# Delta-rule products and value transposes put down later, half pages kept out of the residual's buffers

## The chip, the core and the metric

One core of one Trainium2 chip runs the whole program. TensorE (PE) multiplies matrices, VectorE (DVE) and ScalarE (ACT) do elementwise work, GpSimd (POOL) helps, and SyncE (SP) issues nearly all DMAs between the chip's memory (HBM) and on-chip memory. Each engine runs its own instructions in order and waits on semaphores for the others; a DMA whose buffer is still in use holds up every later DMA of SP. The metric is the device time of one execution, as a median of several.

## The reference

The program is two transformer blocks over x of 1024 tokens by 1024 features, in fp32. The change lies in the first block and in what that block's buffers do later; the first block is, cut to its core:

```python
mod = cond @ w_ada + b_ada                       # cond = silu(c), six rows of 1024
sh_a, sc_a, gt_a, sh_f, sc_f, gt_f = split(mod, 6)
h = x * (1 + sc_a) + sh_a
q, k, v, z, a, b, gl_q, gl_k, gl_v, gl_g, gl_r = split(h @ w_in)
o_dn  = gated_delta_rule(l2(q), l2(k), v, ...)   # 4 heads of 128, chunks of 64
o_gla = gla_attention(...)                       # 4 heads
y = concat(gate(o_dn, z), gate(o_gla, gl_g)) @ w_o
x = layer_norm(ALPHA * x + (1 + gt_a) * y, ln1_g, ln1_b)
h = x * (1 + sc_f) + sh_f
u = causal_dwconv(h @ w_up, conv_w) + conv_b     # 1024 -> 2 * 2816, then 3 taps along time
y = (silu(gate) * val) @ w_down
x = layer_norm(ALPHA * x + (1 + gt_f) * y, ln2_g, ln2_b)
```

The delta rule solves, for each chunk of 64 tokens, a unit lower triangular system with I + M. The kernel inverts the 16x16 diagonal blocks first and then doubles the block size twice.

## The kernel before

**Products.** Every large product in fp32 is done as three products of a rounded high part and a remainder: ACT writes the high part (L430), DVE subtracts it to get the low part (L433, `split`), and PE runs three matmuls (`mm3`, through `mm` at L415; transposes are at L419). Weights come by DMA in blocks of 256 or 512 KB, the modulation's w_ada in pieces of 128x512.

**What sets the order.** The host program writes the instructions with a planner (`Order`). Work is split into generators. `yield t` says that what follows is due t planner microseconds later; a generator that is due goes ahead of the main stream of products. `yield self.need(n)` makes a generator wait until n pages of on-chip memory are free. What comes out is one fixed list of instructions per engine.

**Pages.** `Arena` hands out pages of 1024 columns (`full`) and halves of them (`half`). A caller can name pages that it would rather not have (`away`). In `half`, that list counts only if a new page has to be cut; a half that is already free is handed out, whatever page it is from. Two groups matter here: the eight pages `ypages` (named `y` in the trace), which hold rows of the residual and then of the mixer's output, and five pages `dset`, on which the FFN's product streams its weights.

**Around the change.**
- `mod_rest` (L881) makes eight pieces of the modulation rows while the mixer runs: for a piece, eight loads of w_ada (L891) into three halves, eight accumulating DVE operations (L900, the first L902), and then either a reshaping to columns or a product with a column of ones; for the gate rows the sum goes to HBM (gta_d, gtf_d; L916) through the first of these halves.
- `delta` (L1442) prepares one head, inverts its 16x16 blocks in 15 short pairs of DVE operations (L1541, L1543, L1546), writes the inverse and its transpose to HBM (t_d, L1547; u_d, L1548), and starts `delta_levels` (L1604) for each half of the sequence. That reads both back (L1613, L1614) and doubles the block size with small fp32 matmuls (128x64 results).
- `mix_op` (L1687) claims the `ypages`, loads the mixer's eight rows mix_d (L1695, 512 KB each), and transposes them for the output product.
- `st_up` (L1911) is the FFN's first product, in Strassen steps of twelve matmuls. It keeps four steps of split weights ready in a ring; weights come by L1931 into pages of `dset`, and each pair of weight blocks takes one half page for a temporary: `tmp[q] = A.half(self.dset)` (L1938). ACT copies the result of the first step of a block into a page (L1996), later steps are added by DVE (L1998 to L2007). `unit_out` and the convolution (L2044 to L2049, L2108, L2136) then work on it and store to s_d.
- `res_rows` (L1784) runs beside it as a generator of its own: it builds the residual rows of the second layer norm. Its loop is

```python
        for t in range(8):
            yield self.need(1)
            pg = A.full()
            x, rows = pg.ap, slice(t * P, (t + 1) * P)
            nc.sync.dma_start(x, self.xh_d[rows, :])
            yield 7
            # twice: x *= ln1_g row, yield 3.5, x += ln1_b row, yield 3.5
            nc.sync.dma_start(self.res_d[rows, :], x)
            A.give(pg)
```

(load L1797, DVE L1801 and L1803 twice each, store L1805). The two layer-norm rows hold two pages of their own until the loop ends.

Of the kernel before, what the change touches and what calls it, by code (L numbers as in the profile page):

```python
# [99 lines left out]
class Arena:  # L100
# [14 lines left out]
    def full(self, away=()):  # L115

        for a in (list(away) + self.avoid, self.avoid):
            for i, p in enumerate(self.free):
                if p not in a:
                    return self.free.pop(i)  # L120
        return self.free.pop(0)

    def half(self, away=()):
        if not self.hfree:
            p = self.full(away)
            p.subs = [Page(p.ap[:, 0:512], p, 0), Page(p.ap[:, 512:1024], p, 1)]
            self.hfree += p.subs
        return self.hfree.pop(0)

    def give(self, *xs):  # L130
# [39 lines left out]
def p3(ap, b=P):  # L170
    return ap.rearrange("p (a b) -> p a b", b=b)
# [6 lines left out]
class Down:  # L178
# [23 lines left out]
    def load(self):  # L202
        K = self.K
        A, q = K.A, K.nc.sync
        mine = lambda: [p for p in A.free if p in K.dset]
        while len(self.gp) < 4 and mine():
            pg = A.full([p for p in A.free if p not in K.dset])
            self.gp.append(pg)
            self.gb += [pg.ap[:, 0:512], pg.ap[:, 512:1024]]

        while self.gi < min(len(self.steps), self.at + len(self.gb)):
            c, p, k = self.steps[self.gi]
            q.dma_start(self.gb[self.gi % 8], K.s_d[self.chunks[c][k], :, SLOT[p]])
            self.gi += 1
        while self.want and mine():
            c, x, k = key = self.want.pop(0)
            self.pg[key] = A.full([p for p in A.free if p not in K.dset])
            if x != "t":
                q.dma_start(self.pg[key].ap, self.src(2 * self.chunks[c][k] + (x == "w1")))
        ok = lambda p: p in K.dset and p not in K.dn  # L220
        while not self.want and self.more and any(ok(p) for p in A.free):
            x, f = key = self.more.pop(0)
            pg = K.tail[key] = A.full([p for p in A.free if not ok(p)])
            q.dma_start(pg.ap, K.g_d[f] if x == "g" else self.src(f))
# [86 lines left out]
class Kern:  # L311
# [569 lines left out]
    def mod_rest(self, cond):  # L881
        nc, I, A = self.nc, self.I, self.A
        V = nc.vector
        self.gta_d = self.dram.tile([1, D], F32, name="gta_d")
        self.gtf_d = self.dram.tile([1, D], F32, name="gtf_d")
        self.mcol2 = self.const.tile([P, 16], F32, name="mcol2")
        for c in range(4, 12):
            yield self.need(0, 4)
            ah, *wh = [A.half() for _ in range(4)]
            acc = ah.ap  # L890
            load = lambda k: nc.sync.dma_start(wh[k % 3].ap, I["w_ada"][0, k * P:(k + 1) * P, c * 512:(c + 1) * 512])  # L891
            load(0)
            load(1)
            for k in range(KT):
                yield 5.5
                if k + 2 < KT:
                    load(k + 2)
                a = wh[k % 3].ap
                if k:
                    V.scalar_tensor_tensor(acc, a, cond[:, k:k + 1], acc, op0=OP.mult, op1=OP.add)  # L900
                else:
                    V.tensor_scalar(acc, a, cond[:, 0:1], None, op0=OP.mult)  # L902
            A.give(*wh[1:])
            yield 2
            if c // 2 in (3, 4):
                self.mod_cols(acc, self.mcol2[:, 4 * (c - 6):4 * (c - 5)], 4 * c, 4)
            else:
                dst = self.gta_d if c // 2 == 2 else self.gtf_d
                br = wh[0].ap[0:1, :]
                nc.sync.dma_start(br, I["b_ada"][0:1, c * 512:(c + 1) * 512])  # L910
                yield 2.66
                ps = self.ps()
                self.mm(ps[:1, :], self.ones[:, 0:1], acc, True, True)
                V.scalar_tensor_tensor(br, ps[:1, :], 1.0, br, op0=OP.add, op1=OP.add)
                self.psg(ps)
                nc.sync.dma_start(dst[:, c % 2 * 512:(c % 2 + 1) * 512], br)  # L916
            A.give(ah, wh[0])
            self.mod_done = c
            yield 0.44
# [522 lines left out]
    def delta(self, h, kq, vp):  # L1442
        nc, A, o = self.nc, self.A, self.o
# [9 lines left out]
        for hf in range(2):  # L1453
            yield self.need(0, 7)
            u = {n: A.half() for n in ("kd", "xv", "xk", "qd", "at", "Mn")}
            sqh = A.half()
            sq = p3(sqh.ap)
            U.append(u)
            kd, xv, xk, qd, at, Mn = (p3(u[n].ap) for n in ("kd", "xv", "xk", "qd", "at", "Mn"))
            c0 = hf * 4  # L1460
            hc = slice(h * 8 + c0, h * 8 + c0 + 4)
            tok = lambda c: slice((c0 + c) * P, (c0 + c + 1) * P)
            ss, r = self.sm(), self.sm()

            pq = self.ps()
            for c in range(4):
                self.tr(pq[:, c * P:(c + 1) * P], q_[:, tok(c)])
            S.activation(sqh.ap, pq, AF.Square)
            V.tensor_reduce(ss[:, 4:8], sq, AX.X, OP.add)
            self.psg(pq)  # L1470
            yield 0.93
            pk = self.ps()
            for c in range(4):
                self.tr(pk[:, c * P:(c + 1) * P], k_[:, tok(c)])
            S.activation(sqh.ap, pk, AF.Square)
            S.copy(u["kd"].ap, pk)
            V.tensor_reduce(ss[:, 0:4], sq, AX.X, OP.add)
            self.psg(pk)
            self.rstd(ss, 8, r)

            pg = self.ps()
            for c in range(4):
                g = h * 8 + c0 + c
                self.tr(pg[:, c * P:(c + 1) * P], self.Gc[:, g:g + 1].to_broadcast([P, P]))
            V.tensor_tensor(Mn, p3(pg), bc(self.Gc[:, hc]), OP.subtract)
            S.activation(u["qd"].ap, pg, AF.Exp)
            self.psg(pg)
            mb = lambda m: m[:, None, :].to_broadcast([P, 4, P])
            yield 0.7
            V.scalar_tensor_tensor(at, Mn, 0.0, mb(self.mU), op0=OP.min, op1=OP.add)  # L1490
            V.scalar_tensor_tensor(Mn, Mn, 0.0, mb(self.mL), op0=OP.max, op1=OP.add)
            V.tensor_tensor(qd, qd, p3(q_[:, c0 * P:(c0 + 4) * P]), OP.mult)
            S.activation(u["at"].ap, u["at"].ap, AF.Exp)
            S.activation(u["Mn"].ap, u["Mn"].ap, AF.Exp, scale=-1.0)
            yield 1.5
            u["rq"] = rq = self.sm()
            sb, sn = self.sm(), self.sm()
            br, br2, xkc, nbr2 = sb[:, 0:4], sb[:, 4:8], sn[:, 0:4], sn[:, 4:8]
            V.tensor_scalar(rq[:, 0:4], r[:, 4:8], 128.0 ** -0.5, None, op0=OP.mult)
            V.tensor_mul(br, r[:, 0:4], self.beta[:, hc])  # L1500
            V.tensor_mul(br2, r[:, 0:4], br)
            V.tensor_mul(xkc, br2, self.eG[:, hc])
            V.tensor_scalar(nbr2, br2, -1.0, None, op0=OP.mult)
            V.tensor_tensor(xk, kd, bc(xkc), OP.mult)
            V.tensor_tensor(kd, kd, bc(self.ekd[:, hc]), OP.mult)
            V.tensor_tensor(Mn, Mn, bc(nbr2), OP.mult)
            pv = self.ps()
            for c in range(4):
                self.tr(pv[:, c * P:(c + 1) * P], v_[:, tok(c)])
            V.tensor_tensor(xv, p3(pv), bc(br), OP.mult)  # L1510
            self.psg(pv)
            yield 1.02
            for n, x, dst in ((0, k_, Mn), (1, q_, at)):
                pa = self.ps()
                for c in range(4):
                    t = tok(c)
                    self.mm(pa[:, c * P:(c + 1) * P], k_[:, t], x[:, t], True, True)
                V.tensor_tensor(dst, p3(pa), dst, OP.mult)
                self.psg(pa)
            dst = bass.AP(tensor=md.tensor, offset=md.offset + c0 * CS, ap=[[P, P], [CS, 4], [1, P]])  # L1520
            nc.sync.dma_start(dst, Mn)
            A.give(sqh)
            self.smf += [ss, r, sb, sn]
            yield 0.61
# [79 lines left out]
    def delta_levels(self, h, hf, u, td, ud, ready):  # L1604
        nc, A = self.nc, self.A
# [6 lines left out]
        full = lambda a: bass.AP(tensor=a.tensor, offset=a.offset + c0 * self.CS, ap=[[P, P], [self.CS, 4], [1, P]])  # L1612
        nc.sync.dma_start(Ut, full(ud))  # L1613
        nc.sync.dma_start(Tt, full(td))  # L1614
        yield 6
        c4 = lambda t: t[:, 0:256].rearrange("p (c n b) -> p c n b", c=4, b=b)
        for lev, b in enumerate((16, 32)):

# [1597 lines left out]
```

## Time and profile before

| | |
|---|---|
| median of 3 runs | 2675.36 us (2671.88 to 2675.5) |
| the profiled execution | 2670.58 us, its span 2668.8 us |
| PE busy | 2569.5 us, 96% |
| DVE busy | 1986.2 us, 74% |
| ACT busy | 1280.1 us, 48% |
| POOL busy | 225.7 us, 8% |
| mean granted PE clock | 0.986 |
| HBM | 130 GB/s over the span |

PE is busy for 96% of the span, so its idle gaps and the stretches in which its clock is granted at half are what a change of order can give back or add. In a timeline row the number in brackets is the idle time of the engine just before, and what released it. A row of a transfer is the time at which it is issued, not its duration; the time until it lands is read from what waits for it.

### The profile page before, as it was taken

How to read it: one execution, taken by the hardware profiler on the slowest of the kernel's cores; microseconds unless marked ns; L12 is line 12 of the kernel's file. 1: busy time of each engine (PE TensorE's matmuls, PEld its weight loads, DVE VectorE, ACT ScalarE, POOL GpSimd, SP SyncE). 2: the span in 40 equal slices, each digit the busy share in tenths (PEclk: the TensorE clock that was granted, in tenths of full speed). 3: DMA queues.
4: the chain of work that ended last, by engine and by line, in shares of the span. 5: the costliest groups of instructions: out<-in, count | busy, mean ns of one | idle time of the engine just before them, and what ended most of it. 6: DMA issues, size and time to landing. Idle time of an engine off the chain costs nothing. (4 is left out here: it accounts for less than half of the span.)

```text
span 2668.8 us, 35914 instructions
## 1 busy us (share of the span) xinstructions
PE 2569.5 (96%) x13053; PEld 2098.6 (79%) x13053; DVE 1986.2 (74%) x3407; ACT 1280.1 (48%) x2197; POOL 225.7 (8%) x348
## 2 busy tenths in 40 slices
PE   6999999989999999999989899999999999999998
PEld 5788888879877877788867676779878888888886
DVE  7986576677888888898867775685546866798774
ACT  5433333333545444554357777763544333344443
POOL 1001010100000000000130423210000000000002
PEclk9999799999999999999999999999999999999999
DMA  8433343664443343365211312266114434584531
GB/s 250 145 95 114 89 119 116 201 218 156 119 161 116 122 160 117 135 204 155 96 56 41 86 48 57 69 203 205 50 46 128 154 130 150 183 300 128 177 120 63
DMA packets 298113, 352.34 MB, mean 132 GB/s; under 512 B 32945, under 2 KB 218057, under 8 KB 297937
## 3 DMA queue, kind: packets, MB, share of 16 engines
q1 hardware_dynamic: 297552, 349.90, 41.0%
q8 instruction: 103, 1.69, 0.3%
q14 instruction: 73, 0.60, 0.1%
q10 hardware_dynamic: 385, 0.15, 0.0%
HBM read 248.32 MB, written 97.48 MB: 130 GB/s over the span
## 5 line engine op out<-in xcount | busy, mean ns | idle before, releaser
L415 PE MATMUL b<-oph,wl 128*128 128x512 f32 (+1 forms) x1552 | 619.6, 401 | 9.3 <-ACT oph L670 7.3
L415 PE MATMUL b<-opl,wh 128*128 128x512 f32 (+1 forms) x1552 | 611.7, 394 | 0.0
L415 PE MATMUL b<-oph,wh 128*128 128x512 f32 (+1 forms) x1552 | 608.4, 392 | 0.0
L415 PEld LDWEIGHTS b<-oph,wl 128*128 128x128 f32 x1552 | 292.4, 189 | 76.0 <-ACT oph L670 7.7
L415 PEld LDWEIGHTS b<-oph,wh 128*128 128x128 f32 x1552 | 292.3, 188 | 62.2 <-issue 1.7
L415 PEld LDWEIGHTS b<-opl,wh 128*128 128x128 f32 x1552 | 292.8, 189 | 60.3 <-issue 2.4
L415 PE MATMUL b<-opl,oph 128*128 128x512 f32 x672 | 261.4, 389 | 0.0
L415 PE MATMUL b<-oph 128*128 128x512 f32 x672 | 261.4, 389 | 0.0
L415 PE MATMUL b<-oph,opl 128*128 128x512 f32 x672 | 261.3, 389 | 0.0
L430 ACT CAST oph<-pg 128x512 fp32r<-128x512 f32 (+1 forms) x202 | 125.4, 629 | 240.4 <-PE b L415 204.7
L433 DVE TENSOR_TENSOR opl<-pg,oph 128x512 fp32r<-128x512 f32 (+1 forms) x218 | 149.9, 697 | 66.4 <-ACT oph L430 65.7
L415 PE MATMUL b<-wh,opl 128*128 128x256 f32 (+1 forms) x608 | 197.2, 325 | 0.9 <-DVE opl L433 0.6
L415 PE MATMUL b<-wl,oph 128*128 128x256 f32 (+1 forms) x608 | 193.1, 318 | 0.0
L415 PE MATMUL b<-wh,oph 128*128 128x256 f32 (+1 forms) x608 | 192.6, 317 | 0.0
L433 DVE TENSOR_TENSOR wl<-wf,wh 128x1024 fp32r<-128x1024 f32 (+2 forms) x113 | 141.9, 1255 | 65.2 <-ACT wh L430 63.8
L430 ACT CAST wh<-wf 128x1024 fp32r<-128x1024 f32 (+2 forms) x113 | 121.7, 1077 | 82.5 <-PE b L415 59.1
L430 ACT CAST wh<-y 128x512 fp32r<-128x512 f32 x155 | 96.3, 623 | 111.7 <-PE b L415 97.0
L415 PEld LDWEIGHTS b<-oph,opl 128*128 128x128 f32 x672 | 126.1, 188 | 26.6 <-ACT y L2011 0.2
L415 PEld LDWEIGHTS b<-oph 128*128 128x128 f32 x672 | 126.1, 188 | 26.2
L415 PEld LDWEIGHTS b<-opl,oph 128*128 128x128 f32 x672 | 126.1, 188 | 25.9
L433 DVE TENSOR_TENSOR wl<-y,wh 128x512 fp32r<-128x512 f32 x155 | 105.3, 685 | 41.1 <-ACT wh L430 40.5
L415 PEld LDWEIGHTS b<-wh,opl 128*128 128x128 f32 x608 | 115.5, 190 | 11.3 <-issue 2.2
(1079 smaller groups left out, 4960.9 us busy)
## 6 DMA issues: line engine op xcount, KB each, us to landing
pg<-s_d SPq DMA_DIRECT2D x168, 256.0 KB
wf<-in_w_in_dram SPq DMA_DIRECT2D x48, 512.0 KB
s_d<-pg SPq DMA_DIRECT2D x30, 512.0 KB
s_d<-y SPq DMA_DIRECT2D x28, 512.0 KB
y<-in_ffn_w_up_dram SPq DMA_DIRECT2D x26, 512.0 KB
pa<-in_w_ada_dram SPq DMA_DIRECT2D x47, 256.0 KB
y<-in_w_mlp_in_dram SPq DMA_DIRECT2D x20, 512.0 KB
dn<-in_w_mlp_out_dram SPq DMA_DIRECT2D x18, 512.0 KB
```

The costliest lines, as they stand in the source:

```text
L415: self.nc.tensor.matmul(o, a, b, start=start, stop=stop, **kw)
L430: nc.scalar.copy(hi, src)
L433: (lo_eng or nc.vector).tensor_tensor(out=lo, in0=src, in1=hi.bitcast(F32), op=OP.subtract)
```

## The change

Four edits, all of them in the planner's world; every product and sum stays as it is.

1. `Arena.half` first looks for a free half whose page is not in `away`. If there is none, and a free page outside `away` exists, it cuts that page, and puts the two halves at the front of the list. Only then does it take a half from a page in `away`.
2. `mod_rest` takes its four halves with `away` = `ypages`.
3. `mod_rest` puts its last step 4.5 planner microseconds after the last accumulation, was 2; `delta` gets a `yield 2.5` ahead of the transposes of the values.
4. `delta_levels` puts its first product 9.5 planner microseconds after the loads of u_d and t_d, was 6.

The other callers of `half` that name pages to stay away from, `st_up`'s temporary among them (`dset`), meet the new rule as well.

```diff
     def half(self, away=()):
-        if not self.hfree:
+        for i, p in enumerate(self.hfree):
+            if p.par not in away:
+                return self.hfree.pop(i)
+        if not self.hfree or any(p not in away for p in self.free):
             p = self.full(away)
             p.subs = [Page(p.ap[:, 0:512], p, 0), Page(p.ap[:, 512:1024], p, 1)]
-            self.hfree += p.subs
+            self.hfree[0:0] = p.subs
         return self.hfree.pop(0)
@@ mod_rest
-            ah, *wh = [A.half() for _ in range(4)]
+            ah, *wh = [A.half(self.ypages) for _ in range(4)]
@@ mod_rest, after the last accumulation
-            yield 2
+            yield 4.5
@@ delta, before the transposes of the values
+            yield 2.5
             pv = self.ps()
@@ delta_levels, after the loads of u_d and t_d
-        yield 6
+        yield 9.5
```

Lines of the changed kernel are 3 higher than before, and 4 higher from `delta` on.

The change moves instructions in much of the first block. Three places follow.

**DVE at the inverse of the delta rule's third head.** The short rows (64x4x12 and so on) are steps of the inverse, the copy of 64x256 is its last, after which t_d is written. Before:

```order
L1261 SCALAR_TENSOR_TENSOR pg<-pg,y 128x1024
L1541 TENSOR_TENSOR y<-y 64x3x13
L1294 SCALAR_TENSOR_TENSOR y<-y,pg 128x512
L1543 TENSOR_TENSOR y<-y 64x3x13
L1302 TENSOR_TENSOR pg<-y 128x512
L1541 TENSOR_TENSOR y<-y 64x2x14
L1306 TENSOR_TENSOR smalls<-smalls 128x4
L872 TENSOR_TENSOR pa_105<-pa_105,y 128x512
L1543 TENSOR_TENSOR y<-y 64x2x14
L873 TENSOR_TENSOR pa_105<-pa_105,pa_99 128x512
```

and in the changed kernel, the same steps of the same head:

```order
L876 TENSOR_TENSOR y<-y,pa_99 128x512
L1545 TENSOR_TENSOR pa_106<-pa_106 64x3x13
L1573 TENSOR_TENSOR wl_631<-b_82,wh_630 128x128
L1547 TENSOR_TENSOR pa_106<-pa_106 64x3x13
L436 TENSOR_TENSOR wl_74<-wf,wh_73 128x1024
L1545 TENSOR_TENSOR pa_106<-pa_106 64x2x14
L1547 TENSOR_TENSOR pa_106<-pa_106 64x2x14
L1545 TENSOR_TENSOR pa_106<-pa_106 64x15
L1547 TENSOR_TENSOR pa_106<-pa_106 64x15
L1550 COPY pa_106<-pa_106 64x256
```

The inverse of this head now stands earlier in the program, in a part with fewer wide operations between its steps.

**SP at the last rows of the mixer's output.** gtf_d is the row of the modulation's gate, `y` a page of `ypages`. Before:

```order
L910 DMA y<-in_b_ada_dram 1x512
L944 DMA pa_100<-in_positions_dram 32x256 x4
L463 DMA wf<-in_w_o_dram 128x8x256
L916 DMA gtf_d<-y 1x512
L1695 DMA y<-mix_d 128x1024
```

and in the changed kernel:

```order
L1699 DMA y<-mix_d 128x1024 x4
L894 DMA pa_98<-in_w_ada_dram 128x512
L466 DMA wf<-in_w_o_dram 128x8x256
L894 DMA pa_98<-in_w_ada_dram 128x512
L913 DMA pa_98<-in_b_ada_dram 1x512
L1704 DMA pg<-zg_d 128x512
L1704 DMA pa_105<-zg_d 128x512
L947 DMA pa_98<-in_positions_dram 32x256 x3
L894 DMA pg<-in_w_ada_dram 128x512 x2
L894 DMA pa_103<-in_w_ada_dram 128x512
L919 DMA gtf_d<-pa_98 1x512
```

Before, the last row of mix_d is loaded behind the write of gtf_d, whose source lay in that row's page. Now all eight rows have been issued ahead of it, and gtf_d is written from another page.

**SP and DVE at the residual's rows, in the FFN's first product.** On SP, before, a row of `res_rows` (xh_d in, res_d out) has weight loads and stores of other work between its steps:

```order
L1797 DMA y<-xh_d 128x1024
L1931 DMA y<-in_ffn_w_up_dram 128x8x128 x2
L1805 DMA res_d<-y 128x1024
L1931 DMA y<-in_ffn_w_up_dram 128x8x128
L2049 DMA s_d<-y 128x1024
L1931 DMA pb_5320<-in_ffn_w_up_dram 128x8x128
```

In the changed kernel the first row stands as below, and then the pair of the last two lines comes six times more with nothing between, always on one page, until the eighth row is stored:

```order
L1801 DMA pg<-xh_d 128x1024
L1935 DMA y<-in_ffn_w_up_dram 128x8x128
L1935 DMA pb_5321<-in_ffn_w_up_dram 128x8x128
L1809 DMA res_d<-pg 128x1024
L1801 DMA pg<-xh_d 128x1024
```

On DVE, before, the two pairs of a row stand among splits (L433) and additions of PE's results (b_81, b_82, b_79):

```order
L433 TENSOR_TENSOR wl_4050<-y,wh_4049 128x512
L1801 TENSOR_TENSOR y<-y,pg 128x512 x2
L2005 TENSOR_TENSOR y<-b_81,y 128x512
L433 TENSOR_TENSOR wl_4050<-y,wh_4049 128x512
L1803 TENSOR_TENSOR y<-y,pg 128x512 x2
L2005 TENSOR_TENSOR y<-b_82,y 128x512
L433 TENSOR_TENSOR wl_4050<-y,wh_4049 128x512
L2007 TENSOR_TENSOR pg<-b_79,pg 128x512
```

In the changed kernel the third row stands ahead of one last pair of splits, and rows 4 to 8 follow it, five times the pair of L1805 and L1807, of which the last stands here with what comes behind it:

```order
L1805 TENSOR_TENSOR pg<-pg 128x512 x2
L1807 TENSOR_TENSOR pg<-pg 128x512 x2
L2140 SCALAR_TENSOR_TENSOR pg<-wf,cf,pg 128x1023
L2002 TENSOR_TENSOR pg<-b_77,pg 128x512
L2140 SCALAR_TENSOR_TENSOR pg<-wf,cf,pg 128x1022
L2112 TENSOR_TENSOR pg<-y,pg 128x1024
```

All five rows use the page that the row before has just been stored from. The next split for PE, the addition of PE's result b_77, and ACT's copy of b_81 into a page that a layer-norm row held until then all stand behind the eighth row.

## Rows read from the trace of the kernel before

**Rows 1.** The page: the span, and busy time of the engines.
```profile
span 2668.8 us, 35914 instructions
PE 2569.5 (96%) x13053; PEld 2098.6 (79%) x13053; DVE 1986.2 (74%) x3407; ACT 1280.1 (48%) x2197; POOL 225.7 (8%) x348
```

**Rows 2.** PE's timeline: start, duration (us), line, operation, and idle time before.
```profile
288.85 1.94 PE L415 MATMUL b<-y,wl 128*128 128x64 f32 x8 [4.38 <-DMA y<-u_d]
...
440.88 1.36 PE L415 MATMUL b<-y 128*128 128x64 f32 x8 [3.01 <-DMA y<-u_d]
...
548.03 0.39 PE L415 MATMUL b<-oph,wl 128*128 128x512 f32 x1
548.26 0.39 PE L415 MATMUL b<-opl,wh 128*128 128x512 f32 x1
...
557.25 1.53 PE L415 MATMUL b<-wl,ones 128*1 128x512 f32 x2 [2.58 <-DVE wl L900]
...
570.12 5.03 PE L419 MATMUL b<-ident,y 128*128 128x128 f32 x24 [5.12 <-DMA y<-mix_d]
```

**Rows 3.** Windows: length, busy PE, PEld, DVE, ACT, POOL, PEclk, DMA, GB/s.
```profile
289.00:299.00 10.00, 10.00 (x43) 9.52 (x44) 1.20 (x3) 0.81 (x3) 0.00 (x0) 0.50 0.26 72
299.00:316.00 17.00, 16.99 (x99) 15.69 (x99) 1.97 (x5) 3.92 (x9) 0.53 (x1) 0.52 0.00 1
441.00:451.00 10.00, 10.00 (x48) 8.87 (x49) 3.33 (x6) 1.34 (x3) 0.00 (x0) 0.66 0.53 173
571.00:577.00 6.00, 6.00 (x39) 6.00 (x39) 5.97 (x10) 3.19 (x6) 0.00 (x0) 0.69 0.54 175
```

**Rows 4.** SP's timeline at the third head and at the mixer's last row.
```profile
281.23 0.59 SPq L1547 DMA_DIRECT2D t_d<-y  x1
...
561.73 0.32 SPq L916 DMA_DIRECT2D gtf_d<-y  x1
566.54 0.34 SPq L1695 DMA_DIRECT2D y<-mix_d  x1
```

**Rows 5.** DVE's timeline in the third head's inverse.
```profile
272.75 0.49 DVE L902 TENSOR_SCALAR y<-pa,cond 128x512 f32<-128x512 f32 x1 [1.41 <-DMA pa<-in_w_ada_dram]
...
275.75 1.21 DVE L1261 SCALAR_TENSOR_TENSOR pg<-pg,y 128x1024 f32<-128x1024 f32 x1
...
279.75 0.69 DVE L873 TENSOR_TENSOR pa<-pa,pa 128x512 f32<-128x512 f32 x1
```

**Rows 6.** SP's timeline at residual rows, in the FFN's first product.
```profile
749.52 0.33 SPq L1797 DMA_DIRECT2D pg<-xh_d  x1
...
838.36 0.34 SPq L1805 DMA_DIRECT2D res_d<-y  x1
841.40 0.37 SPq L1931 DMA_DIRECT2D y<-in_ffn_w_up_dram  x1
...
866.31 0.91 SPq L1797 DMA_DIRECT2D y<-xh_d  x1
...
995.08 0.34 SPq L1805 DMA_DIRECT2D res_d<-wf  x1
998.96 0.37 SPq L1931 DMA_DIRECT2D wf<-in_ffn_w_up_dram  x1
```

**Rows 7.** DVE's timeline at the same rows.
```profile
755.76 1.29 DVE L1801 TENSOR_TENSOR pg<-pg 128x512 f32<-128x512 f32 x2 [0.33 <-DMA pg<-xh_d]
...
795.24 1.28 DVE L1803 TENSOR_TENSOR y<-y,pg 128x512 f32<-128x512 f32 x2
...
871.80 0.69 DVE L1801 TENSOR_TENSOR y<-y,pg 128x512 f32<-128x512 f32 x1 [3.04 <-DMA y<-xh_d]
```

**Rows 8.** PE's timeline at two of the FFN's last units.
```profile
1053.31 0.50 PE L415 MATMUL b<-oph,wl 128*128 128x512 f32 x1 [0.78 <-DVE wl L433]
...
1058.05 0.51 PE L415 MATMUL b<-tsh,wl 128*128 128x512 f32 x1 [1.72 <-DVE wl L433]
```

## Prediction

> **What bounds the kernel now.** I read the busy shares first. PE works for 2569.5 of 2668.8 us, DVE for 74% of the span, ACT for less [rows 1]. A large product puts out a 128x512 matmul every 0.23 us (548.03 to 548.26) [rows 2]. So the time is PE's own work plus PE's gaps plus the stretches at half clock. No matmul is added or dropped by the change, so I look only at the gaps and the clock. The waits of PE come next, then the windows around them, then the queue that feeds them.
>
> In the delta-rule stage PE waits 4.38 us for u_d at the third head and 3.01 us at the fourth, then 2.58 us for the last accumulation of a gate row, then 5.12 us for the eighth row of the mixer's output [rows 2]. Behind three of the four gaps the granted clock is low: 0.50 and 0.52 over 10 and 17 us, 0.66 over 10, 0.69 over 6 [rows 3]. A stretch of length t at a clock g does the work of g x t, so these cost (1 - 0.50) x 10 + (1 - 0.52) x 17 = 13.2 us, 0.34 x 10 = 3.4 us and 0.31 x 6 = 1.9 us.
>
> **Part 1: the mixer's last row.** Before, its load goes out at 566.54, behind the write of gtf_d at 561.73 from the same page, and lands 3.6 us later, when the transposes start at 570.12 [rows 2, 4]. With the mod pieces off the y pages, the order has all eight loads ahead of that write. Gain: 5.12 us and the 1.9 us of clock behind it. What comes next there is w_o, of which a block is issued ahead of gtf_d in both orders, so I put no new wait in its place.
>
> **Part 2: level products.** The new due time does not do evenly what its number says. Counted in the two orders, the matmuls between the write of t_d and the first level product were 30, 30, 30 and 39 for the four heads and are now 28, 36, 30 and 60. At the third head t_d is written at 281.23 and its product starts at 288.85, 7.6 us later [rows 2, 4]. Thirty matmuls of 0.23 us cover 6.8 us of it, so with DVE on time only 0.8 us would be left. The other 3.6 us come from DVE, which reached the end of the inverse late: one wait of 1.41 us for w_ada, and wide operations of 0.7 to 1.2 us between the last steps [rows 5]. In the new order that inverse has one modulation operation where six stood, and in its last steps a 128x1024 split and short rows. I take DVE as on time there: 3.6 us gained, 0.8 kept. At the fourth head sixty matmuls cover 13 us against a round trip of about 7.6: its 3.01 us go. With these gaps go their low stretches, 13.2 and 3.4 us. The first two heads keep their margins, and their gaps, below 1 us each, I leave as they are.
>
> **Part 3: the ones product.** Its accumulation still waits for the last w_ada load, which in the new order stands behind four mix rows and a w_o block. Half of 2.58 us is taken, 1.3, with bounds of 0 and 2.6, since neither order says when that load lands.
>
> Sum of the gains: 5.1 + 1.9 + 3.6 + 3.0 + 13.2 + 3.4 + 1.3 = 31.5 us. At the least only parts that the order settles come: 5.1 + 1.9 + 3.0 + 3.4 = 13.4. At the most, with all of the two stalls, 34.
>
> **Part 4: residual rows in the FFN.** This is where I expect the time to go. The temporary of each pair of weight blocks asks for a half away from dset; under the new rule a whole page is cut for it although a free half exists. Pages run short, and main waits for one. Each time res_rows gives its page back, its next row takes it again before main does, so the rows run one behind the other on one page while PE's next steps are written behind them. Before, every row had weight loads, splits and PE work between its load, its arithmetic and its store. Now rows 4 to 8 stand at one place of PE's order, with 7 matmuls, 1.6 us, between the third row's store and the place where PE must wait: for a split behind the eighth row on DVE, and for ACT's copy into a layer-norm page.
>
> A row costs a load, four DVE operations and the store, in series, since the next load needs the page. The load takes 6.2 us from its issue at 749.52 to 755.76, or 5.5 from 866.31 to 871.80, in this stage; the equally large mix row, issued alone, 3.6 [rows 2, 4, 6, 7]. A store holds its page 3.0 us (838.36 to 841.40) to 3.9 (995.08 to 998.96) [rows 6]. Two pairs of DVE operations take 1.29 + 1.28 = 2.6 us [rows 7]. One row is then between 3.6 + 3.0 + 2.6 = 9.2 and 6.2 + 3.9 + 2.6 = 12.7 us. SP is itself held by this chain and sends nothing else, so the lone load is the nearest row: I take 3.6 + 3.2 + 2.6 = 9.4. Five rows make 47, less 1.6 of cover: 45.4; bounds 44.4 and 61.9. After a gap of that length the clock will be low for a while: between 1.7 us (as behind the mix row) and 13.2 (as at the third head), 3 taken.
>
> The Trainium skill, "DMA: Bandwidth & Descriptors", section "Anatomy of one DMA", says that a transfer pays about 2.0 us of fixed cost, mostly the receipt that its last byte has landed, plus bytes / 436e9. By that, as an estimate, 512 KB take 3.2 us and five rows 5 x (3.2 + 3.2 + 2.6) = 45 us; the page gives its fit for another path of issue than SP's, and the rows above agree with it only where a load runs alone.
>
> **Part 5: the units behind it.** In the new order seven units have their gating and convolution rows ahead of the split that PE needs next. Before, only the last ones did, and there PE waited 0.78 and 1.72 us, together 2.5 [rows 8]. I count six of the seven as new, at 1.5 us each: 9; nothing at the least, 11 at the most, since DVE may have caught up during the long wait.
>
> **Sum.** -31.5 + 45.4 + 3 + 9 = +25.9 us on the profiled execution of 2670.58, so 2696.5. The median of the runs lies 4.8 us above that execution, and the time asked for is a median: 2701 us.
>
> **Rivals.**
> A. *The early gains do not come.* If DVE is late again at the third head, 3.6 + 13.2 us of the gains go, and with the ones product another 1.3: +44, 2719 us. For it: the margin there is 30 matmuls as before. Against it: the lighter DVE.
> B. *The chain runs at the stage's own latencies.* Loads of 6.2 and stores of 3.9 us give 61.9 in place of 45.4: +42, 2717 us. Weight loads issued ahead of the chain may still be under way in its first row, less so in the last.
> C. *Other side: the rows overlap.* If the five rows were on different pages, the loads could go out together and only DVE's 5 x 2.6 = 13 us would hold PE, less the 1.6: -31.5 + 11.4 + 9 = -11 us, 2664 us. The sign turns where five rows, less 1.6, cost what the rest gives back (31.5 - 9 - 3 = 19.5): at 4.2 us a row. Against it: a load and a store alone are 6.6 us, and the order shows load and store of one page in turn.
> D. *Gains and chain nearly cancel.* Gains at 34, chain at 44.4, clock at 1.7, units at nothing: +12, 2688 us, still slower. To come within 0.2% of before, a row would then have to cost some 7.5 us.
>
> **How the numbers follow.** A change of this kernel under 0.2%, some 5 us, cannot be told from none. The forecast holds 0.62 (its own range 2690 to 2712), A 0.13, B 0.13, C 0.06, D 0.06. Forecast, A and B are slower. Of C two thirds are faster and a third within 0.2%; of D a third is within 0.2% and the rest slower. That makes faster 0.04, same 0.04, slower 0.92. The range runs from 2685, a little under D's sum, to 2722, just above A and B.
>
> **What the changed profile would show.** Right: no wait on mix_d of 5 us, no clock near 0.5 behind the third head, and between about 720 and 800 us of the span one stretch of some 45 us in which PE is idle, DVE does only L1805 and L1807 in fours, and SP alternates xh_d and res_d every 9 to 10 us; waits on the split L436 in most units behind it. A total a little under PE's busy time of before says that the low clock is gone. Wrong: rows on SP that follow each other by less than 5 us, or a chain with PE at work beside it, would refute part 4; a gap of 3 us or more before the third head's level product would refute part 2.

## The result, and the profile after

| | before | changed |
|---|---|---|
| median of runs taken side by side | 2675.06 us (4 runs) | 2713.13 us (4 runs, 2710.71 to 2722.01) |
| profiled execution, its span | 2670.58, 2668.8 us | 2710.71, 2708.9 us |
| PE busy | 2569.5 us | 2561.0 us |

The changed kernel is slower: ratio 1.0159, 95% interval 1.0136 to 1.0181. The medians differ by 38.1 us, the profiled executions by 40.1. PE's busy time even fell by 8.5 us, so all of the loss is idle time of PE. Its waits over the whole span, in the changed kernel (line, what it waited for, us in total, times, longest):

```profile
PE b L418 <- ACT pg L2000: 41.5, 1, 41.5
PE b L418 <- DVE wl L436: 20.2, 18, 1.7
...
PE b L418 <- DMA y<-u_d: 5.3, 2, 3.8
...
PE b L418 <- DVE y L1573: 2.5, 2, 2.3
PE b L418 <- DVE pa L1339: 2.1, 2, 1.2
PE b L422 <- DVE pa L1319: 2.1, 1, 2.1
...
PE b L418 <- DVE wh L903: 0.7, 1, 0.7
```

One wait of 41.5 us is new, and is as large as the whole loss. The waits on splits (L436) have grown as well; before, the same line stood at

```profile
PE b L415 <- DVE wl L433: 6.6, 5, 2.2
```

The wait on mix_d of [rows 2] is not in the list at all, and the one for the last accumulation (L903) is 0.7 us, was 2.58.

Behind the long wait stand the residual's rows. SP's timeline of the changed kernel there, without the rows between:

```profile
765.52 0.32 SPq L1809 DMA_DIRECT2D res_d<-pg  x1
768.14 0.32 SPq L1801 DMA_DIRECT2D pg<-xh_d  x1
774.12 0.32 SPq L1809 DMA_DIRECT2D res_d<-pg  x1
776.74 0.32 SPq L1801 DMA_DIRECT2D pg<-xh_d  x1
...
808.18 0.32 SPq L1809 DMA_DIRECT2D res_d<-pg  x1
```

and DVE's:

```profile
771.59 1.29 DVE L1805 TENSOR_TENSOR pg<-pg 128x512 f32<-128x512 f32 x2 [2.96 <-DMA pg<-xh_d]
772.80 1.29 DVE L1807 TENSOR_TENSOR pg<-pg 128x512 f32<-128x512 f32 x2
780.01 1.29 DVE L1805 TENSOR_TENSOR pg<-pg 128x512 f32<-128x512 f32 x2 [5.92 <-DMA pg<-xh_d]
```

and PE's, at its end and at the next unit:

```profile
808.81 0.80 PE L418 MATMUL b<-tsh,wl 128*128 128x512 f32 x1 [41.55 <-ACT pg L2000]
...
842.70 0.50 PE L418 MATMUL b<-oph,wl 128*128 128x512 f32 x1 [0.79 <-DVE wl L436]
...
847.43 0.51 PE L418 MATMUL b<-tsh,wl 128*128 128x512 f32 x1 [1.73 <-DVE wl L436]
```

Read together: a store goes out at 765.52, the load into the same page 2.62 us later, DVE starts 3.45 us after that, and the next store follows at 774.12. Five rows take from 765.52 to 808.18, 8.53 us each, and PE's first matmul comes 0.63 us after the last store. Where before DVE did these rows among PE's own work [rows 7], it now does nothing else. The pair of waits at 842.70 and 847.43 answers to [rows 8]; it now comes in most units.

The lead that the first block gave can be read from one landmark, the first FFN store, whose row in the kernel before is

```profile
734.47 0.34 SPq L2049 DMA_DIRECT2D s_d<-pg  x1
```

and in the changed kernel

```profile
718.72 0.34 SPq L2053 DMA_DIRECT2D s_d<-pg  x1
```

15.7 us earlier. So in this pair of executions the sum is a gain of 15.7 us up to that store and a loss of some 56 us behind it.

### The profile page after: what moved, and what is told of

It reads as the page before. It is cut to its first block, busy times and chain, and to the rows that moved or that the text cites. A ratio compares the mean times of both kernels' runs of the same rounds, so it can differ in the third digit from the quotient of the medians.

```text
span 2708.9 us, 35910 instructions
## 1 busy us (share of the span) xinstructions
PE 2561.0 (95%) x13053; PEld 2084.9 (77%) x13053; DVE 1991.0 (73%) x3407; ACT 1277.6 (47%) x2197; POOL 229.4 (8%) x348
## 5 line engine op out<-in xcount | busy, mean ns | idle before, releaser
L418 PEld LDWEIGHTS b<-oph,wl 128*128 128x128 f32 x1552 | 292.0, 189 | 82.7 <-DVE wl L436 10.3
L433 ACT CAST oph<-pg 128x512 fp32r<-128x512 f32 x202 | 125.5, 629 | 236.9 <-PE b L418 200.2
L436 DVE TENSOR_TENSOR opl<-pg,oph 128x512 fp32r<-128x512 f32 (+1 forms) x208 | 143.4, 701 | 66.6 <-ACT oph L433 64.7
L436 DVE TENSOR_TENSOR wl<-wf,wh 128x1024 fp32r<-128x1024 f32 (+2 forms) x108 | 138.8, 1285 | 64.4 <-ACT wh L433 52.7
L433 ACT CAST wh<-wf 128x1024 fp32r<-128x1024 f32 (+2 forms) x108 | 118.7, 1099 | 90.5 <-PE b L418 61.4
L418 PE MATMUL b<-tsh,wl 128*128 128x512 f32 x272 | 108.7, 402 | 54.6 <-ACT pg L2000 41.5
L433 ACT CAST wh<-y 128x512 fp32r<-128x512 f32 x159 | 98.6, 622 | 128.7 <-PE b L418 107.2
L436 DVE TENSOR_TENSOR wl<-y,wh 128x512 fp32r<-128x512 f32 x159 | 110.0, 696 | 66.1 <-ACT wh L433 65.9
```

The lines of the kernel that those rows point to most:

```text
L418: self.nc.tensor.matmul(o, a, b, start=start, stop=stop, **kw)
L433: nc.scalar.copy(hi, src)
L436: (lo_eng or nc.vector).tensor_tensor(out=lo, in0=src, in1=hi.bitcast(F32), op=OP.subtract)
```

## The experiments

Theory: one call for a half page, the FFN's temporary, cuts the last free page; the residual's rows then run one behind the other on the page that is left, and PE stands still. The ratio given with each is to the kernel before on the same chip.

**One call back on the old rule.** `half0` is the old `half`, word for word.

```diff
-                tmp[q] = A.half(self.dset)
+                tmp[q] = A.half0(self.dset)
```

> The changed kernel, with one call back on the old rule: the FFN's temporary takes any free half, as before. Theory (the rows queue up because this one call cuts the last free page): no chain, PE's wait of 41.5 us gone and with it the waits on splits in most units; what is left is the lead of 15 us that the changed kernel had at the first FFN stores, so 2655 to 2664 us. Rival 1 (the chain comes from the shifted times of the streams, whichever page the temporary has): a chain of rows stays, 2700 us or more. Rival 2 (the lead is lost again later, by page shortage elsewhere): no chain, but 2670 to 2680 us.

Measured: 2659.03 us, ratio 0.9955 (0.994 to 0.997). PE's waits in the FFN, 700 to 1150 us:

```profile
PE b L425 <- DVE wl L443: 7.1, 5, 2.7
PE b L425 <- ACT pg L2014: 4.0, 6, 0.7
```

11.1 us in all, with no chain. The changed kernel less this one call is faster than before by some 12 us, so the chain and the units behind it are the whole loss. Both rivals fall. The early lead is real as a median, but its size differs from execution to execution: the profiled one, among the slower of the ten at 2664.24 us, has the first FFN store only 4.6 us ahead of the kernel before, although PE's and SP's orders are those of the changed kernel up to the FFN.

```profile
729.91 0.34 SPq L2060 DMA_DIRECT2D s_d<-pg  x1
```

**The new rule of `half` alone.** Edit 1 on the kernel before.

> The kernel before with the new rule of half alone; modulation rows and due times as before. Theory, as the prediction put it (the rule alone cuts a page although a half is free): a chain, 2715 to 2730 us. Refined theory (the rule bites only when the free half at that call is from the pages to stay away from, which depends on the history that the other edits set): the planned order shows no chain, 2675 within 5 us.

Measured: 2686.42 us, 1.0061 (1.004 to 1.0082), and no chain. My theory as the prediction put it is refuted in its generality: the rule does not cut a page at every temporary. The refined form is right about the chain and wrong about the time. The other streams that ask for halves away from y pages get other pages too, and that alone moved the first block for the worse, as PE's waits from 350 to 700 us show, 28.3 us in all against 14.0 before:

```profile
PE b L418 <- DMA pa<-u_d: 5.9, 1, 5.9
PE b L422 <- DVE pa L1723: 5.1, 5, 3.5
PE b L422 <- DMA y<-mix_d: 4.7, 1, 4.7
PE b L418 <- DVE pa L674: 3.5, 1, 3.5
```

What the rule meets is a matter of the arena's state. Written out by the planner at the first product's third and fourth temporary (free pages in dset and elsewhere, and the free half's page):

```
kernel before   3rd: free 0 in dset, 1 elsewhere, no half   -> cuts the other page
                4th: free 1 in dset, 0 elsewhere, half of a page elsewhere -> takes the half
changed kernel  3rd: free 1 in dset, 0 elsewhere, no half   -> cuts the dset page
                4th: free 0 in dset, 1 elsewhere, half of a dset page      -> cuts the last page
```

From there each of the residual's rows 2 to 8 finds one free page, and two halves lie idle. Before, those rows found three to five.

**One page cut in the kernel before.** At the fourth temporary alone, the free half is hidden for the call.

```diff
+                self.ntmp = getattr(self, "ntmp", 0) + 1
+                kept = A.hfree
+                if self.ntmp == 4:
+                    A.hfree = []
                 tmp[q] = A.half(self.dset)
+                if self.ntmp == 4:
+                    A.hfree = A.hfree + kept
```

> The kernel before with one difference: the FFN's fourth temporary is made to cut a page although a free half lies there. Theory (one page less at that call is enough for the chain): rows 2 to 8 queue up on one page, PE idle for some 40 us in one piece, 2715 to 2735 us. Rival (the shortage needs the other edits as well): under 2690 us.

Measured: 2727.97 us, 1.0211 (1.0182 to 1.0239), 56 us slower. PE's waits from 700 to 1150 us and two of SP's stores:

```profile
PE b L415 <- ACT pg L2002: 42.2, 1, 42.2
PE b L415 <- DVE wl L433: 18.5, 15, 1.7
```

```profile
780.37 0.32 SPq L1805 DMA_DIRECT2D res_d<-pg  x1
...
823.17 0.32 SPq L1805 DMA_DIRECT2D res_d<-pg  x1
```

Five rows in 42.8 us, 8.56 each, one gap of 42.2 us and the pair of waits in the units behind. One page at one call is enough, with none of the four edits. The price of the chain by itself, 56 us, less the 12 us that the edits otherwise give, leaves 44, close to the 38 to 42 us by which the changed kernel is slower.

**Main first.** The page stays cut, but a row lets main claim ahead of it.

```diff
             nc.sync.dma_start(self.res_d[rows, :], x)
             A.give(pg)
+            yield 1
```

> The changed kernel with one planner microsecond between a residual row's give of its page and its next claim, so that the main stream, waiting for a page, gets it first. The page that is cut stays cut. Theory (the loss is the order of claims on a short supply, not the shortage as such): no chain of five rows, the wait of 41.5 us gone, 2658 to 2672 us. Rival (with one page less the weights come late in any order): 2690 us or more.

Measured: 2663.05 us, 0.9978 (0.9966 to 0.999). PE's waits in the FFN are 14.7 us and SP's timeline has other work between the rows:

```profile
775.17 0.32 SPq L1809 DMA_DIRECT2D res_d<-pg  x1
777.78 0.32 SPq L1801 DMA_DIRECT2D pg<-xh_d  x1
786.82 0.34 SPq L1809 DMA_DIRECT2D res_d<-pg  x1
...
817.87 0.32 SPq L1801 DMA_DIRECT2D y<-xh_d  x1
```

The shortage as such costs a few us: the ratio is 0.9978 against 0.9955 in the first experiment, with intervals that just overlap, and the waits are 14.7 us against 11.1. What costs is who gets the page: in the planner a ready stream goes ahead of main, also when main has waited longer.

**Rule and one due time.** Edit 1, and in `mod_rest` 4.5 for 2.

> The kernel before with the new rule of half and the modulation rows' later last step (4.5, was 2), neither the pages of the modulation rows nor the level products' due time changed. Its planned order has six rows of the residual in a row. Theory (rule and history together make the chain, and these two edits are enough): one PE gap of 40 us or more, 2715 to 2740 us. Rival (the chain needs the modulation rows off the residual's pages): under 2695 us.

Measured: 2751.48 us, 1.0315 (1.0291 to 1.0339), the slowest of all, with one gap of 47.71 us:

```profile
849.12 0.79 PE L418 MATMUL b<-tsh,wl 128*128 128x512 f32 x1 [47.71 <-ACT wf L1999]
```

A due time in the first block's modulation rows decides whether the FFN, behind it, loses 48 us: with the rule alone there is no chain, with this due time there is. The range that I gave was too low by 11 us, since the first block is slow here too: the first FFN store goes out at 753.60 us, 19.1 later than before.

**Rule and pages.** Edits 1 and 2, due times as before.

> Edits 1 and 2 together (new rule of half, modulation rows off the residual's pages), all due times as before. The planned order has no chain. Theory: the wait for the mixer's last row (5.1 us) and the low clock behind it (1.9) go, the rest of the delta stage shifts by a few us either way: 2660 to 2672 us. Rival (the due times carry the early gain): 2672 to 2680 us.

Measured: 2678.54 us, 1.0032 (1.0015 to 1.0049). The wait on mix_d is gone, as expected, but the time is not; my range was missed and the rival's time came. In its place in the first block stand waits such as

```profile
PE b L422 <- DVE pg L1723: 3.4, 3, 2.0
PE b L422 <- ACT y L645: 2.9, 2, 2.1
PE b L418 <- DMA y<-u_d: 2.8, 1, 2.8
PE b L418 <- DMA pa<-u_d: 2.5, 1, 2.5
```

These are of the fastest of the ten executions (2668.13 us, 10 us under the median), and its waits from 150 to 700 us sum to 21.3 us against 23.7 before. So they do not explain why the median is 7 us longer; that stays open.

**Due times alone.** Edits 3 and 4 (with the transposes' 2.5) on the kernel before.

> The kernel before with the three due times alone; half and the modulation rows' pages as before. The planned order has no chain; PE's work between the write of t_d and the first level product at the fourth head is 5.4 us, counted by shape, against 8.3 before. Theory (that work is the cover of a round trip of some 10 us): the fourth head waits 4 to 6 us, was 3.0, the wait for the mixer's last row stays if its page is still shared, 2668 to 2685 us. Rival (the due times carry the early gain): 2664 us or less.

Measured: 2664.68 us, 0.9982 (0.997 to 0.9995): faster by about 5 us, under my range of 2668 to 2685 and 0.7 us above the rival's 2664. The theory missed, and the reason that I gave failed: the fourth head's product starts with no wait for u_d at 444.24, 8.0 us behind the write of t_d at 436.20. The count of work in the order, 5.4 us, assumes that DVE writes t_d on time; here it was ahead. The wait on mix_d went too, though the modulation rows took their halves by the old rule. Edits 1 and 2 alone cost 7 us, the due times alone gain 5, and all four without the chain gain 12: the effects do not add up.

**Level products later still.** The first experiment's kernel, 11 for 9.5, and then 8:

```diff
-        yield 9.5
+        yield 11
```

> The changed kernel with the temporary on the old rule and level products due after 11 planner microseconds, was 9.5. By shape PE's work between the write of t_d and the fourth head's first level product is 14.9 us, was 9.5. Theory: the fourth head's wait (3.4 to 3.8 us) and the low clock that can follow it go, the other heads keep about 1 us: 2640 to 2655 us, and less spread than the runs with 9.5. Rival (something behind it, the products' own chain of steps, waits as long): 2655 to 2662 us.

Measured: 2659.35 us, 0.9965 (0.9945 to 0.9985), 12 runs from 2650.26 to 2675.7. The fourth head's wait is gone, but the others grew: the second head's product starts after 3.08 us of wait, the third's after 2.46 (0.72 and 1.29 in the first experiment), and the granted clock is 0.86 from 200 to 250 us and 0.88 from 250 to 300.

```profile
218.79 1.18 PE L425 MATMUL b<-pg,y 128*128 128x64 f32 x8 [3.08 <-DMA pg<-u_d]
...
285.40 1.10 PE L425 MATMUL b<-y 128*128 128x64 f32 x8 [2.46 <-DMA y<-u_d]
```

The spread became wider, not narrower. No gain over 9.5 can be told, since the intervals overlap: the rival's time, by another cause than the rival's.

> The changed kernel with the temporary on the old rule and level products due after 8 planner microseconds, was 9.5. PE's work between the write of t_d and the first level product, counted by shape in the planned order, is 6.6, 5.6, 7.5 and 12.9 us for the four heads; with 9.5 it is 6.4, 6.4, 6.6 and 9.5, with 11 it is 6.3, 5.7, 6.6 and 14.9. Theory (a gap is a round trip of 7.3 to 10 us less this work): about 1 us of wait at the first head, 2 at the second, under 1 at the third, none at the fourth, 2648 to 2658 us. Rival (any gap of 2 us can bring a long stretch of half clock, so the second head's takes back what the fourth gives): 2657 to 2665 us, no better than with 9.5.

Measured: 2661.63 us, 0.9972 (0.9958 to 0.9986). The fourth head waits 0.24 us, the third 3.72, where I expected under 1, and behind that one the clock is low (0.56 from 274 to 304 us).

```profile
274.67 1.97 PE L425 MATMUL b<-pa,pg 128*128 128x64 f32 x8 [3.72 <-DMA pa<-u_d]
...
449.38 1.10 PE L425 MATMUL b<-pa,pa 128*128 128x64 f32 x8 [0.24 <-DMA pa<-u_d]
```

The rival's time again. A due time for all heads moves the gap from one head to another. The kernel of the first experiment, at 0.9955 of the one before, beats that one and the changed one; 11 and 8 (0.9965 and 0.9972) cannot be told from it.

## Why the prediction was right, point by point

**Part 1, the mixer's last row (gain 7.0): came.** No wait on mix_d, and from 560 to 700 us PE is busy for 138.61 of 140 us at a clock of 1.00.

**Part 2, level products (gain 23.2): the third head came, the fourth did not.** The rows of the changed kernel for the two heads, PE's and then SP's:

```profile
260.42 0.39 PE L418 MATMUL b<-oph,wh 128*128 128x512 f32 x1
262.33 1.10 PE L418 MATMUL b<-y,pg 128*128 128x64 f32 x8 [1.52 <-DMA y<-u_d]
...
440.92 0.39 PE L418 MATMUL b<-pa,pg 64*128 64x64 f32 x4
445.13 1.97 PE L418 MATMUL b<-y 128*128 128x64 f32 x8 [3.82 <-DMA y<-u_d]
```

```profile
253.01 0.59 SPq L1551 DMA_DIRECT2D t_d<-pa  x1
...
434.69 0.59 SPq L1551 DMA_DIRECT2D t_d<-pa  x1
...
436.38 1.33 SPq L1704 DMA_DIRECT2D pg<-zg_d  x1
438.96 0.36 SPq L1618 DMA_DIRECT2D pa<-t_d  x1
439.37 0.50 SPq L1618 DMA_DIRECT2D y<-t_d  x1
439.97 0.45 SPq L1617 DMA_DIRECT2D y<-u_d  x1
```

The third head waits 1.52 us (0.8 forecast), and in this execution the long stretch of half clock behind it is gone. That the wait came out near the forecast is in part luck: the round trip from t_d to the product was 9.3 us (253.01 to 262.33), not 7.6, and PE had 7.8 us of work behind t_d, not 6.8, so that two errors nearly cancel.

At the fourth head the failed step is "sixty matmuls cover 13 us". 32 of the sixty are products of 64x64, of which the trace shows four in 0.22 us, so the sixty are at most 9.5 us by shape; and t_d went out late against PE, which had only 6.6 us of work left then (434.69 to 441.31). On the other side the round trip was 10.4 us (434.69 to 445.13), not 7.6: u_d's load goes out 5.3 us behind t_d, 3.8 before, with a zg_d row ahead of it whose issue takes 1.33 us, and the product starts 5.2 us after that load's issue, 3.9 before. PE waited 3.82 us, more than the 3.01 before.

**Part 3, the ones product (gain 1.3): came, 1.9.** The wait is 0.7 us.

**New waits in the first block (none forecast).** The DVE waits L1339 and L1319 of the first fence were not there before, and those on L1573 are longer. From 150 to 720 us, PE's waits other than the ones of parts 1 to 3 are 14.3 us, against 8.6 before: 5.7 more. So of the forecast's 31.5 go 6.4 for the fourth head, whose gains did not come, 0.8 for its longer wait, 0.3 for its low clock (some 7.3 us of work at half clock between 445.13 and 453.3, which cost 3.7; 3.4 before), 5.7 for the new waits and 0.7 for the third head, and 0.6 is added for the ones product: 18.2, against 15.7 read at the landmark. The other 2.5 were not traced.

**Where the early gain lies.** By PE's waits alone the changed kernel is only 3.3 us better from 150 to 720 us (20.4 against 23.7). Most of the 15.7 us is clock that was low in the one execution of before and high in this one. The first experiment's kernel, with the same program up to the FFN, waits even less there, 18.1 us, but lost the clock at the fourth head and stood at 4.6 us. So the sum in the prediction, which took a stretch of low clock as the price of its gap, rests there on one execution; the median over ten, 12 us, is the better measure of the early gain.

**Part 4, the chain (45.4 forecast, 41.5 measured): right in place and kind, and nearly in size.** The five rows took 42.7 us, PE had 1.7 us of work behind the third store (1.6 forecast), and 0.6 passed behind the last one. A row took 8.53 us, below my lower bound of 9.2: the store held its page for 2.62 us and the load took 3.45 to DVE's start, both less than the shortest rows of before (3.0 and 3.6) [rows 2, 4, 6]. DVE took 2.5, as forecast. By the fit in the Trainium skill ("DMA: Bandwidth & Descriptors", "Anatomy of one DMA"), which the page gives for another path of issue than SP's, the estimate for 512 KB is 3.2 us for either; the trace has the load close to it and the store well below. What was wrong is the reason in words: not every temporary cuts a page although a half is free. Of the first four the first and the fourth did, the fourth took the last free page, and only in the state that the other edits had made. The prediction could be right because it read the finished order, and did not depend on why it came about. Behind the gap the granted clock is 0.51 over the 3 us from 808.8 to 811.8 and full from there on, which cost 1.5 us; 3 were forecast. (The prediction gives the clock behind the mix row as 1.9 us in part 1 and as 1.7 in part 4; its rows give 1.9. In rival D a change of 5 us needs a row of 7.8 us, not some 7.5.)

**Part 5, the units (9 forecast, 10.3 measured).** PE's waits from 720 to 1150 us other than the long one are 20.9 us (19.6, 1.0 and 0.3), against 10.6 in the same stage before.

**The sum.** -15.7 + 41.5 + 10.3 + 1.5 = 37.6, and the profiled executions differ by 40.1. Of the rest, 1.7 us arose behind the FFN: a later landmark, the first addition of L2075, is 38.4 us late. What makes these few us was not settled. Forecast +25.9: the early gains were half of what I took, 15.8 us short, as rival A said, though not where it said it, and a chain shorter by 3.9 us made up for a part. The median, 2713, lies just above the forecast's own range of 2690 to 2712 and nearer to A's 2719 than to 2701. The direction and the mechanism of the loss were foreseen; the size was met only because the whole range, 2685 to 2722, had taken in A and B.

## What to carry to other kernels

Where a planner sets the order, read the finished order for a resource that is claimed twice in a row by the same stream: its rows then cost their whole round trip in series, and a main stream that waits for the same resource stands still. A rule for choosing buffers is no local edit; test it where buffers are scarcest, and let the stream that feeds the bounding engine claim first. Price the cover of a wait by the shape of the matmuls, not by their number, add what is queued ahead of the transfer on its queue, and count the cover from when the write really goes out.

## What the runs showed of the hardware

The same gap does not cost the same clock each time. The changed kernel and that of the first experiment have the same program up to the FFN, and wait 3.82 and 3.42 us at the fourth head. Behind it, from 440 to 480 us, the first has

```profile
440.00:480.00 40.00, 34.53 (x249) 29.97 (x248) 22.62 (x43) 11.31 (x29) 2.62 (x4) 0.87 0.44 132
```

and the second

```profile
440.00:480.00 40.00, 35.07 (x158) 30.45 (x159) 13.82 (x27) 7.00 (x20) 1.36 (x3) 0.53 0.32 98
```

(PEclk is the third number from the end): 0.13 of 40 us lost against 0.47, 5 us against 19, of which some 1.5 in each fell while PE stood idle. A third execution of that program up to the FFN, in the run with main first, waits 2.2 us there and has 0.83 over the same 40 us. So a low stretch in one profile, such as that of 27 us in [rows 3], is not a fixed price of its gap. The Trainium skill ("TensorE: Matmul & The Clock Gate", "What's actually happening") has the slow clock as the default and activity as what lifts it; both executions were busy for 35 of these 40 us and were lifted at different times, at 453.3 and 479.4 us. It also shows in the spread: the ten runs of the first experiment's kernel go from 2653.44 us at a mean clock of 0.992 to 2665.96 at 0.986, and those of the kernel before from 2661.44 at 0.990 to 2677.28 at 0.984. What decides in which execution the clock stays low was not tested.
